# The Down product of a one-layer encoder block in Strassen form: a new table of visits in which no pair is read twice, and a last visit with evictions in an order of its own

## The chip, the cores and the metric

The kernel runs on one core of a Trainium2 chip. The metric is the device time of one execution in microseconds (us). Engines are called by their names in the profile: PE is TensorE's matmul, PEld its weight load, DVE VectorE, ACT ScalarE, POOL GpSimd and SP SyncE, which here only issues DMAs; a "q" behind a name (SPq) is that engine's queue of instructions.

## The reference

One layer over 512 tokens of width 2048, in float32. The part that matters is the last line of the layer and the final norm; the mixers and the attention to memory come before them and are not touched.

```python
for l in range(DEPTH):            # DEPTH is 1
    ...
    hm = rmsnorm(x, g_mlp[l])
    x = x + jnp.square(jax.nn.relu(hm @ w_up[l])) @ w_down[l]
return rmsnorm(x, g_final)
```

`w_up` is 2048 x 8192, `w_down` 8192 x 2048. Up is the first of the two products, Down the second.

## The kernel before, in words

All matmuls take float32 operands that were split in two float32r parts, hi and lo, and add three products of them (hi hi, hi lo, lo hi). The program is written by a planner: tasks are Python generators, each with a planned clock, and the order in which they issue on the five engines is fixed when the program is built (`step`, `until`, `spawn`). So each engine runs one written list in its order, and an instruction whose input is late holds up everything behind it on that engine.

Up and Down are both done in Strassen form with seven products instead of eight: `ORDER` names them p1, q6, p7, q4, p2, q5, p3. The work is cut in **units**, 128 for Up and 128 for Down. A unit has one weight block: three DMAs on SP (lines 1461 to 1465) and one DMA on POOL that adds onto what the first brought (line 1470), two adds of 256 columns on DVE, and the split of seven 256-column pieces by `hi_lo`: a cast on ACT (1024 columns, then 768) and a subtraction on DVE (the same two). Two such sets of pieces exist (`hl`), and four raw blocks (`ring`), so the weights of a unit are fetched four units ahead. PE then runs 7 products x 6 matmuls = 42 matmuls of 256 columns (`strassen_pe`, `one_product`, line 308); the first four products need the 1024 piece, the others the 768 one.

**Up** has 16 groups g of 8 units. After the last unit of a group `gen_up_out` takes the seven products out of their PSUM banks into the buffer `G`, squares and scales, forms the seven sums that Down needs (the rows of two **pairs**, 2g and 2g+1) in `G` as well, and writes them to `tp_dram` in DRAM (line 1598). The next group's evictions write `G` again, so they wait until these writes have read it.

**Down** contracts over 32 pairs for each of four output groups `ng`. The pairs come back from `tp_dram` by four DMAs of 224 KB each (`gen_load_t`, line 1646) into eight places of `big`, and are split there by one cast on ACT and one subtraction on DVE, both 128x1792. Since eight places hold eight pairs, Down goes in **visits** (ng, first pair, last pair): a visit runs one unit per pair, its seven products stay in seven of the eight banks, and at its end `gen_down_out` adds them into `CB[ng]`, which was loaded with the residual (`gen_load_res`, line 1669): one copy on ACT and eleven adds of 512 columns on DVE. While these run, the next visit's products take the banks in the order in which they come free. `pace(n)` behind a unit allows n more pair quarters to be fetched. Behind the ends of the last four visits (`FINAL`) `gen_square` squares the finished group on ACT and sums it on POOL, and `gen_out` does the final norm and the output. In the last visit q5 and p3 of all its pairs are put off to the end (`LATE`), from pieces kept in a free place of `big`; so a unit of the last visit has five products, 30 matmuls.

The visits of before have 4, 6, 8, then twelve of 8 pairs, then 2, 8 and 4; pairs 0 and 1 are read a second time as pairs 32 and 33, so 34 pairs are loaded (`NLOAD`).

## Time and profile before

| | us |
|---|---|
| median of 3 runs | 2350.24 (2349.97 to 2350.58) |
| the profiled execution | 2349.65 |
| its span, first to last instruction | 2347.9 |
| PE busy in the span | 2259.0 (96%) |
| DVE busy | 1681.3 (72%) |
| ACT busy | 1077.4 (46%) |
| mean granted clock of PE | 0.989 |

PE is busy for nearly the whole span, so what can be gained are its gaps and the time in which it runs at the lower clock. In a timeline a row has the start and the length in us, the engine, the line, what is written and read, the count of instructions that were merged, and in brackets the engine's idle time before it and what ended it.

### The profile page before, as it was taken

How to read it: one execution, taken by the hardware profiler on the slowest of the kernel's cores; microseconds unless marked ns; L12 is line 12 of the kernel's file. 1: busy time of each engine (PE TensorE's matmuls, PEld its weight loads, DVE VectorE, ACT ScalarE, POOL GpSimd, SP SyncE). 2: the span in 40 equal slices, each digit the busy share in tenths (PEclk: the TensorE clock that was granted, in tenths of full speed). 3: DMA queues.
4: the chain of work that ended last, by engine and by line, in shares of the span. 5: the costliest groups of instructions: out<-in, count | busy, mean ns of one | idle time of the engine just before them, and what ended most of it. 6: DMA issues, size and time to landing. Idle time of an engine off the chain costs nothing.

```text
span 2347.9 us, 41841 instructions
## 1 busy us (share of the span) xinstructions
PE 2259.0 (96%) x16056; PEld 2168.0 (92%) x16056; DVE 1681.3 (72%) x2645; ACT 1077.4 (46%) x1506; POOL 388.3 (17%) x477
## 2 busy tenths in 40 slices
PE   8999999999999999899999999998899999999986
PEld 8999999998888787799999999998899999999986
DVE  7678543447734557978687776877887878878777
ACT  6542433345533446654454544444444444444453
POOL 3110010113002101311111111111111111111131
PEclk9999999999999999999999999999999999999998
DMA  5323222231243434688878788789978888887963
GB/s 172 103 88 95 68 75 82 68 104 46 90 160 100 157 116 156 165 223 231 230 204 246 198 229 225 197 240 258 299 215 238 214 235 219 218 229 206 237 164 108
DMA packets 273770, 405.42 MB, mean 173 GB/s; under 512 B 24193, under 2 KB 176785, under 8 KB 273313
## 3 DMA queue, kind: packets, MB, share of 16 engines
q1 hardware_dynamic: 235392, 334.44, 44.0%
q0 software_dynamic: 36944, 67.21, 17.1%
q8 instruction: 125, 2.05, 0.3%
q10 hardware_dynamic: 1232, 1.09, 0.1%
q14 instruction: 77, 0.62, 0.1%
HBM read 364.90 MB, written 37.75 MB: 171 GB/s over the span
## 4 chain that ended last, share of the span: by engine, by line
PE 67%; DVE 15%; DMA 9%; issue 4%; POOL 2%; ACT 1%; SPq 1%; DVEq 0%; ACTq 0%; POOLq 0%
PE bank L308 34%; PE bank L303 31%; DVE fb L139 8%; DVE hl L139 5%; DMA tp_dram<-fb 3%; DMA fb<-in_w_up_dram 3%; DVE big L139 2%; PE bank L328 2%; POOL fb L139 2%; DMA fb<-in_w_dn_dram 1%; ACT hl L139 1%; DMA big<-tp_dram 1%; SPq L1463 0%; ACT fb L139 0%; SPq L1461 0%
## 5 line engine op out<-in xcount | busy, mean ns | idle before, releaser
L308 PE MATMUL bank<-big,hl 128*128 128x256 f32 x10704 | 1314.9, 285 | 55.1 <-DVE hl L139 26.2
L308 PEld LDWEIGHTS bank<-big,hl 128*128 128x128 f32 x10704 | 1300.6, 193 | 69.1 <-DVE hl L139 32.5
L139 ACT CAST hl<-fb 128x1024 fp32r<-128x1024 f32 (+4 forms) x699 | 641.1, 926 | 911.9 <-PE bank L308 369.3
L139 DVE TENSOR_TENSOR hl<-fb,hl 128x768 fp32r<-128x768 f32 (+5 forms) x698 | 746.4, 1082 | 426.1 <-ACT hl L139 425.4
L303 PE MATMUL bank<-hl,big 128*128 128x384 f32 (+4 forms) x2916 | 525.2, 330 | 8.0 <-ACT big L139 7.0
L303 PEld LDWEIGHTS bank<-hl,big 128*128 128x128 f32 x2916 | 479.4, 189 | 19.0 <-ACT big L139 7.0
L139 DVE TENSOR_TENSOR fb<-fb 128x256 f32<-128x256 f32 (+3 forms) x779 | 401.5, 526 | 84.3 <-DMA fb<-in_w_up_dram 57.8
L303 PE MATMUL bank<-big,hl 128*128 128x512 f32 (+1 forms) x1192 | 296.1, 390 | 0.0
L139 POOL TENSOR_TENSOR fb<-fb 128x128 f32<-128x128 f32 (+5 forms) x203 | 155.7, 788 | 710.0 <-ACT fb L139 286.2
L303 PEld LDWEIGHTS bank<-big,hl 128*128 128x128 f32 x1192 | 222.2, 188 | 43.3
L1470 POOL DMA_DIRECT2D fb<-in_w_dn_dram x128 | 110.6, 866 | 551.2 <-DMA fb<-in_w_dn_dram 196.7
L1470 POOL DMA_DIRECT2D fb<-in_w_up_dram x128 | 110.7, 865 | 540.1 <-DVE hl L139 211.3
L139 DVE TENSOR_TENSOR fb<-fb,bank 128x512 f32<-128x512 f32 x234 | 156.9, 682 | 42.3 <-DMA tp_dram<-fb 24.3
L139 ACT ACTIVATE fb<-fb 128x512 f32<-128x512 f32 (+2 forms) x144 | 116.6, 814 | 70.9 <-DVE fb L139 50.0
L303 PE MATMUL bank<-big 128*128 128x256 f32 (+2 forms) x534 | 113.2, 327 | 2.1 <-DVE big L139 1.2
L303 PEld LDWEIGHTS bank<-big 128*128 128x128 f32 x534 | 87.1, 188 | 10.1 <-DVE big L139 2.5
L139 ACT CAST big<-bank 128x512 fp32r<-128x512 f32 (+2 forms) x119 | 61.2, 540 | 56.6 <-PE bank L328 28.4
L139 ACT CAST big<-big 128x1792 fp32r<-128x1792 f32 x34 | 57.5, 1691 | 56.5 <-DMA big<-tp_dram 50.4
L139 DVE TENSOR_TENSOR big<-bank,big 128x512 fp32r<-128x512 f32 (+1 forms) x102 | 62.7, 642 | 25.5 <-ACT big L139 25.4
L139 DVE TENSOR_TENSOR big<-big 128x1792 fp32r<-128x1792 f32 x34 | 68.7, 2020 | 3.6 <-ACT big L139 3.6
L328 PE MATMUL bank<-cs,fb 128*128 128x128 f32 x384 | 60.2, 275 | 8.9 <-POOL fb L139 3.5
L328 PEld LDWEIGHTS bank<-cs,fb 128*128 128x128 f32 x384 | 46.3, 140 | 17.2 <-POOL fb L139 5.8
(90 smaller groups left out, 727.0 us busy)
## 6 DMA issues: line engine op xcount, KB each, us to landing
fb<-in_w_up_dram SPq DMA_DIRECT2D x256, 256.0 KB, 5.0
fb<-in_w_dn_dram SPq DMA_DIRECT2D x256, 256.0 KB, 4.9
fb<-in_w_up_dram POOLq DMA_DIRECT2D x128, 256.0 KB, 6.3
fb<-in_w_dn_dram POOLq DMA_DIRECT2D x128, 256.0 KB, 6.0
fb<-in_w_in_dram SPq DMA_DIRECT2D x80, 384.0 KB, 3.0
big<-tp_dram SPq DMA_DIRECT2D x136, 224.0 KB, 5.5
fb<-in_w_out_dram SPq DMA_DIRECT2D x32, 512.0 KB, 3.3
fb<-in_w_up_dram SPq DMA_DIRECT2D x128, 128.0 KB, 5.5
```

The costliest lines, as they stand in the source:

```text
L139: r = fn(*args, **kw)
L303: nc.tensor.matmul(out, lhsT, rhs, start=start, stop=stop)
L308: nc.tensor.matmul(out, lhsT, rhs, start=start, stop=stop, skip_group_check=True)
L328: nc.tensor.transpose(out, in_, ident)
L1470: nc.gpsimd.dma_start(s31, src[:, 256:768], accum_op=OP.add)
```

## The change

Four things are changed in Up's writes and in Down. The seven sums of an Up group are written to `tp_dram` by two DMAs of 896 KB, one behind the other, where before there were four (two of 512 KB and two of 384 KB) with a planned 4.5 us between them. The table of visits is another one, of 18 visits as before, and loads 32 pairs; the first visits have 4, 4, 6, 8, 6 and 8 pairs, the last four 10, 8, 4 and 6. The pace of the pair loads and of the residual loads is adapted. The last visit puts off two products of 6 pairs (before of 4), and has an eviction of its own (`gen_last_out`), in which the sums for the first half of the columns come first.

```diff
--- before.py
+++ after.py
@@ -1488,16 +1488,16 @@
         flag.add(("sa", i))
         while ("pe", i - 2) not in flag:
             yield 0
-        j = i - (nu - 4)
+        j = i - (nu - NLAST)
         if j < 0:
             yield from hi_lo(hi[:, 1024:1792], lo[:, 1024:1792], r[:, 1024:1792])
             flag.add(("sb", i))
             return
         yield from hi_lo(hi[:, 1536:1792], lo[:, 1536:1792], r[:, 1536:1792])
         flag.add(("sb", i))
-        while ("pe", nu - 11) not in flag:
-            yield 0
-        k = big[:, PAIR * 2 + 1024 * j : PAIR * 2 + 1024 * j + 1024]
+        while ("pe", first_s + 128 + sum(b - a for _, a, b in VISITS[:-3]) + 1) not in flag:
+            yield 0
+        k = big[:, 1024 * j : 1024 * j + 1024]
         yield from hi_lo(k[:, 0:512], k[:, 512:1024], r[:, 1024:1536])
         flag.add(("kept", j))
 
@@ -1592,12 +1592,8 @@
         sums([c(4), c(5), c(6), c(7)], c(0), c(1), c(2), c(3), dve)
         yield rt(G)
         x = G[:, 512:4096].rearrange("p (r m c) -> p r m c", r=7, m=2)
-        for a, b in ((0, 4), (4, 7)):
-            for m in range(2):
-                dst = tp_dram[2 * g + 1 - m][:, 256 * a : 256 * b].rearrange("p (r c) -> p r c", r=b - a)
-                nc.sync.dma_start(dst, x[:, a:b, m, :])
-                if g < 15:
-                    yield plan.clk["pe"] + 4500.0
+        for m in range(2):
+            nc.sync.dma_start(tp_dram[2 * g + 1 - m].rearrange("p (r c) -> p r c", r=7), x[:, :, m, :])
         flag.add(("t", g))
 
     def up_units(g):
@@ -1619,12 +1615,12 @@
 
 
 
-    VISITS = [(0, 0, 4), (1, 0, 6), (2, 0, 8)]
-    VISITS += [(v % 4, 2 * v - 4, 2 * v + 4) for v in range(3, 15)]
-    VISITS += [(1, 30, 32), (3, 26, 34), (0, 28, 32)]
+    VISITS = [(0, 0, 4), (1, 0, 4), (2, 0, 6), (3, 0, 8), (0, 4, 10), (1, 4, 12)]
+    VISITS += [(v % 4, 2 * v - 6, 2 * v + 2) for v in range(6, 14)]
+    VISITS += [(2, 22, 32), (3, 24, 32), (1, 28, 32), (0, 26, 32)]
     FINAL = (14, 15, 16, 17)
     LATE = ("q5", "p3")
-    NLOAD = 34
+    NLOAD, NLAST = 32, 6
     paced = [0]
 
     def pace(n):
@@ -1668,7 +1664,7 @@
                     src = xs_dram[n : n + 2, :, 256 * t : 256 * t + 256].rearrange("e p c -> p e c")
                     nc.sync.dma_start(dst.rearrange("p (e c) -> p e c", e=2), src)
                     plan.issue("dma", 100.0, [dst], [], 4000)
-                    yield plan.clk["pe"] + (1500.0 if ng == 0 else 4500.0)
+                    yield plan.clk["pe"] + (1500.0, 4500.0, 7000.0, 7000.0)[ng]
             flag.add(("res", ng))
 
     def gen_down_out(ng, st):
@@ -1716,6 +1712,42 @@
         free("p3")
         flag.add(("fin", id(st), 0, 1))
 
+    def gen_last_out(ng, st):
+
+        (c11, c12), (c21, c22) = CB[ng]
+        e, u2, u3 = (fslot(6144 + 512 * i) for i in range(3))
+        while not all(splits[nu - 1 - u].done for u in range(NLAST)):
+            yield 0
+
+        def add(dst, x, op=OP.add):
+            dve.tensor_tensor(dst, dst, x, op=op)
+
+        yield from product(st, "p1")
+        act.copy(e, st["p1"])
+        yield from product(st, "q6")
+        yield rt(e)
+        dve.tensor_tensor(u2, e, st["q6"], op=OP.subtract)
+        add(c11, e)
+        yield from product(st, "p7")
+        dve.tensor_tensor(u3, u2, st["p7"], op=OP.add)
+        yield from product(st, "q4")
+        add(c21, st["q4"], OP.subtract)
+        add(c21, u3, OP.subtract)
+        flag.add(("fin", id(st), 1, 0))
+        yield from product(st, "p2")
+        add(c11, st["p2"])
+        flag.add(("fin", id(st), 0, 0))
+        banks_f.put(*(st[r] for r in ORDER[:5]))
+        add(c22, u3, OP.subtract)
+        add(c12, u2)
+        yield from product(st, "q5")
+        add(c22, st["q5"])
+        flag.add(("fin", id(st), 1, 1))
+        add(c12, st["q5"], OP.subtract)
+        yield from product(st, "p3")
+        add(c12, st["p3"])
+        flag.add(("fin", id(st), 0, 1))
+
     def down_index(p, ng):
         if p < 28:
             return 16 * (p // 4) + 4 * ng + p % 4
@@ -1740,16 +1772,19 @@
                     elif v in FINAL:
                         spawn(gen_out(0, st), True)
                         spawn(gen_out(1, st), True)
-                    spawn(gen_down_out(ng, st), True)
+                    spawn(gen_down_out(ng, st) if v != FINAL[-1] else gen_last_out(ng, st), True)
                 strassen_pe(i, st, TP[s], j == 0, j == n - 1, ORDER[:5] if v == FINAL[-1] else ORDER)
                 if v == FINAL[-1] and j == n - 1:
                     until(lambda: ("kept", j) in flag)
                     for x, r in enumerate(LATE):
                         for u in range(n):
-                            k = big[:, PAIR * 2 + 1024 * u : PAIR * 2 + 1024 * u + 1024]
+                            k = big[:, 1024 * u : 1024 * u + 1024]
                             one_product(st, r, k[:, 0:512], k[:, 512:1024], 256 * x, TP[s0 + u],
                                         PRODUCTS[r][1], u == 0, u == n - 1)
-                pace(2 if v == 0 or (v == 1 and j < 2) else 1)
+                if v in (1, 2, 4, 14):
+                    pace((2 if j < 4 else 0) if v in (1, 14) else (2 if j < 2 else 1))
+                elif v > 0:
+                    pace(1)
             return run
 
         return [Unit(w_dn[down_index((s0 + j) % 32, ng)], 1024, pe(j)) for j in range(n)]
@@ -1785,7 +1820,7 @@
         sq = [fslot(4096 + 1024 * t + 512 * m) for m in range(2)]
         rs = rstd_l[:, 2 * t : 2 * t + 2]
         last = VISITS[FINAL[-1]][0]
-        while ("sqd", FINAL[-2]) not in flag or not all(splits[nu - 1 - u].done for u in range(4)):
+        while ("sqd", FINAL[-2]) not in flag or not all(splits[nu - 1 - u].done for u in range(NLAST)):
             yield 0
         b = None
         for x, m in enumerate((1, 0)):
```

The first place in the program is SP's list in the middle of an Up group. Its rows before, with the three DMAs of each unit's weights (lines 1461 to 1465) between the writes of `G`:

```order
L1598 DMA tp_dram<-fb 128x4x256 x2
L1461 DMA fb<-in_w_up_dram 128x2x256
L1463 DMA fb<-in_w_up_dram 128x512
L1465 DMA fb<-in_w_up_dram 128x256
L1461 DMA fb<-in_w_up_dram 128x2x256
L1463 DMA fb<-in_w_up_dram 128x512
L1465 DMA fb<-in_w_up_dram 128x256
L1598 DMA tp_dram<-fb 128x3x256
L1461 DMA fb<-in_w_up_dram 128x2x256
L1463 DMA fb<-in_w_up_dram 128x512
L1465 DMA fb<-in_w_up_dram 128x256
L1598 DMA tp_dram<-fb 128x3x256
```

and of the changed kernel at the same place:

```order
L1596 DMA tp_dram<-fb 896x1x256 x2
L1461 DMA fb<-in_w_up_dram 128x2x256
L1463 DMA fb<-in_w_up_dram 128x512
L1465 DMA fb<-in_w_up_dram 128x256
L1461 DMA fb<-in_w_up_dram 128x2x256
L1463 DMA fb<-in_w_up_dram 128x512
L1465 DMA fb<-in_w_up_dram 128x256
```

All 1792 KB of the group's sums now stand ahead of the weights of the units that follow; before, two writes of 384 KB stood behind the second and the third of these units.

The second place is DVE's list at the end of the second visit (rows `fb<-fb,bank` take a product out, rows `hl<-fb,hl` are the splits of a unit's weights, `fb<-fb 128x256 x2` the adds of one). Before, where that visit has 6 pairs:

```order
L139 TENSOR_TENSOR fb<-fb 128x512
L139 TENSOR_TENSOR fb<-fb,bank_64 128x512
L139 TENSOR_TENSOR fb<-fb 128x512
L139 TENSOR_TENSOR fb<-fb,bank_68 128x512
L139 TENSOR_TENSOR fb<-fb 128x512
L139 TENSOR_TENSOR fb<-fb,bank_63 128x512
L139 TENSOR_TENSOR fb<-fb 128x512
L139 TENSOR_TENSOR fb<-fb,bank_66 128x512
L139 TENSOR_TENSOR hl<-fb,hl 128x1024
L139 TENSOR_TENSOR fb<-fb,bank_70 128x512 x2
L139 TENSOR_TENSOR fb<-fb,bank_67 128x512
```

and of the changed kernel, where it has 4 (the first two adds of the eviction stand just ahead of these rows; `big<-big 128x1792` splits pair 4):

```order
L139 TENSOR_TENSOR fb<-fb 128x512
L139 TENSOR_TENSOR fb<-fb,bank_68 128x512
L139 TENSOR_TENSOR fb<-fb 128x512
L139 TENSOR_TENSOR fb<-fb 128x256 x2
L139 TENSOR_TENSOR fb<-fb,bank_63 128x512
L139 TENSOR_TENSOR fb<-fb 128x512
L139 TENSOR_TENSOR fb<-fb,bank_66 128x512
L139 TENSOR_TENSOR fb<-fb,bank_70 128x512 x2
L139 TENSOR_TENSOR fb<-fb,bank_67 128x512
L139 TENSOR_TENSOR fb<-fb 128x256 x2
L139 TENSOR_TENSOR big<-big 128x1792
L139 TENSOR_TENSOR hl<-fb,hl 128x1024
```

Before, the 1024 piece of the unit after next (the second of the new visit) stood behind the eighth add; now it stands behind all eleven, two pairs of adds for weights and the split of a pair. The splits of pairs 4 and 5, which stood behind the eviction of the first visit in the list of before, have moved here.

The third place is DVE's list where the last visit begins, with the eviction of the visit ahead of it. Before:

```order
L139 TENSOR_TENSOR fb<-fb 128x512
L139 TENSOR_TENSOR fb<-fb,bank_68 128x512
L139 TENSOR_TENSOR fb<-fb 128x512
L139 TENSOR_TENSOR fb<-fb,bank_63 128x512
L139 TENSOR_TENSOR fb<-fb 128x512
L139 TENSOR_TENSOR fb<-fb,bank_66 128x512
L139 TENSOR_TENSOR fb<-fb 128x512
L139 TENSOR_TENSOR fb<-fb,bank_70 128x512
L139 TENSOR_TENSOR hl<-fb,hl 128x1024
L139 TENSOR_TENSOR fb<-fb,bank_67 128x512 x2
L139 TENSOR_TENSOR fb<-fb,bank_69 128x512
```

and of the changed kernel (the first add of the eviction stands just ahead of these rows; `big<-fb,big` keeps a piece for the end):

```order
L139 TENSOR_TENSOR fb<-fb,bank_68 128x512
L139 TENSOR_TENSOR fb<-fb 128x512
L139 TENSOR_TENSOR fb<-fb,bank_63 128x512
L139 TENSOR_TENSOR fb<-fb 128x512
L139 TENSOR_TENSOR fb<-fb 128x256 x2
L139 TENSOR_TENSOR fb<-fb,bank_66 128x512
L139 TENSOR_TENSOR fb<-fb 128x512
L139 TENSOR_TENSOR big<-fb,big 128x512
L139 TENSOR_TENSOR fb<-fb,bank_70 128x512
L139 TENSOR_TENSOR fb<-fb,bank_67 128x512 x2
L139 TENSOR_TENSOR fb<-fb,bank_69 128x512
L139 TENSOR_TENSOR hl<-fb,hl 128x1024
```

Here too the 1024 piece has moved behind all eleven adds, and behind two more steps.

## Rows read from the trace of the kernel before

**Rows 1.** Stretch, length, busy of PE, PEld, DVE, ACT, POOL, PEclk, DMA share, GB/s.
```profile
1088.00:1592.00 504.00, 493.13 (x4053) 490.44 (x4051) 383.73 (x540) 240.16 (x266) 83.51 (x98) 0.99 0.83 221
1592.00:1750.00 158.00, 142.74 (x1130) 139.22 (x1129) 132.21 (x174) 75.42 (x76) 22.93 (x27) 0.98 0.91 262
...
2240.00:2327.00 87.00, 75.56 (x588) 73.76 (x587) 68.76 (x94) 43.99 (x72) 31.73 (x32) 0.94 0.44 107
```

**Rows 2.** PE's waits in these three stretches: total us, times, longest.
```profile
PE bank L308 <- DVE fb L139: 10.8, 10, 3.2
...
PE bank L308 <- DVE hl L139: 8.3, 6, 3.4
PE bank L308 <- DVE fb L139: 6.9, 10, 1.8
...
PE bank L308 <- DVE hl L139: 9.2, 4, 5.6
PE bank L308 <- DVE fb L139: 1.6, 3, 0.6
```

**Rows 3.** The same columns as rows 1, in 8 us at the end of an Up group.
```profile
1463.00:1471.00 8.00, 6.49 (x31) 6.49 (x32) 6.99 (x11) 4.48 (x6) 0.86 (x1) 0.57 0.48 92
```

**Rows 4.** Timeline around the end of that Up group, SPq, DVE and PE.
```profile
1441.21 0.98 SPq L1598 DMA_DIRECT2D tp_dram<-fb  x2
...
1460.21 0.89 DVE L139 TENSOR_TENSOR fb<-fb 128x256 f32<-128x256 f32 x2 [3.45 <-DMA fb<-in_w_up_dram]
...
1463.77 1.48 DVE L139 TENSOR_TENSOR fb<-fb,bank 128x512 f32<-128x512 f32 x2 [2.67 <-DMA tp_dram<-fb]
...
1464.51 1.86 PE L308 MATMUL bank<-big,hl 128*128 128x256 f32 x7 [3.16 <-DVE fb L139]
```

**Rows 5.** DVE's waits in the first stretch, 1088 to 1592 us.
```profile
DVE fb L139 <- DMA fb<-in_w_up_dram: 49.1, 34, 3.4
...
DVE fb L139 <- DMA tp_dram<-fb: 24.3, 12, 4.1
```

**Rows 6.** DMAs issued near 1385, 1441, 1446, 1626: count, size, us to landing.
```profile
fb<-in_w_up_dram SPq DMA_DIRECT2D x2, 256.0 KB, 3.5
...
tp_dram<-fb SPq DMA_DIRECT2D x2, 512.0 KB, 5.9
...
fb<-in_w_up_dram SPq DMA_DIRECT2D x2, 256.0 KB, 7.3
...
tp_dram<-fb SPq DMA_DIRECT2D x1, 384.0 KB, 9.6
```

**Rows 7.** Timeline where Down begins: DVE, ACT and PE.
```profile
1635.34 1.48 DVE L139 TENSOR_TENSOR fb<-fb,bank 128x512 f32<-128x512 f32 x2 [5.73 <-DMA big<-tp_dram]
...
1668.99 2.02 DVE L139 TENSOR_TENSOR big<-big 128x1792 fp32r<-128x1792 f32 x1
...
1671.75 1.69 ACT L139 CAST big<-big 128x1792 fp32r<-128x1792 f32 x1 [9.60 <-DMA big<-tp_dram]
...
1672.20 4.06 PE L308 MATMUL bank<-big,hl 128*128 128x256 f32 x20 [3.44 <-DVE hl L139]
```

**Rows 8.** Timeline at the end of a later visit: first add, eighth's follower, PE.
```profile
2236.29 0.69 DVE L139 TENSOR_TENSOR fb<-fb 128x512 f32<-128x512 f32 x1
...
2241.92 1.22 DVE L139 TENSOR_TENSOR hl<-fb,hl 128x1024 fp32r<-128x1024 f32 x1
...
2244.39 1.81 PE L308 MATMUL bank<-big,hl 128*128 128x256 f32 x13 [0.45 <-DVE fb L139]
```

**Rows 9.** Timeline where the last visit begins: first add, next 1024 piece.
```profile
2298.05 0.68 DVE L139 TENSOR_TENSOR fb<-fb 128x512 f32<-128x512 f32 x1
...
2303.71 1.22 DVE L139 TENSOR_TENSOR hl<-fb,hl 128x1024 fp32r<-128x1024 f32 x1
```

**Rows 10.** Timeline of the tail: sums of squares on PE, first scalings on DVE.
```profile
2326.82 4.93 PE L303 MATMUL bank<-ones,fb 128*128 128x2 f32 x40
...
2332.32 3.67 DVE L139 TENSOR_TENSOR fb<-fb,bank 128x512 f32<-128x512 f32 x6 [0.37 <-PE bank L328]
```

## The prediction, made before the changed kernel was run

> **What bounds the kernel now.** I read the busy times by stretch first, then PE's waits in each, then the timeline at the places where the longest stand. PE is busy for 493.13 of 504 us in Up's main part, 142.74 of 158 where Down begins, 75.56 of 87 at the end [rows 1]. Up's 4053 matmuls in 493.13 us give 0.122 us each, so a unit of 42 takes 5.1 us. What is lost there stands in PE's waits [rows 2]: 10.8 us in ten gaps in Up, 8.3 + 6.9 = 15.2 where Down begins, 9.2 + 1.6 = 10.8 at the end. All are put down to DVE: "DVE hl" means that the split of a unit's weights was late, "DVE fb" that a bank was not yet taken out. With a long gap the granted clock goes to half: in the 8 us around one it is 0.57 and PE makes 31 matmuls [rows 3], which at 0.122 us are 3.8 us of work in the 6.5 us after the gap, so 2.7 lost. DVE is 76% busy in Up but 84% (132.21 of 158) where Down begins [rows 1], so there a gap is not only a wait but a lack of DVE time. I make the sum against the profiled execution, 2349.65 us, which is 0.6 under the median of the three runs.
>
> **Up's writes.** The ten gaps of Up stand at group ends. At the one of 3.16 us DVE's row that takes out the next products had waited 2.67 us for a write of the group before, and just ahead of it an add of weights 3.45 us for its DMA [rows 4]. Over the stretch DVE waited 24.3 us in 12 such waits for writes, 2.0 each, and 49.1 us in 34 for weights [rows 5]; the latter delayed no split that PE stood waiting for, since every wait of PE there is for a bank.
>
> In the new list all 1792 KB are issued where the first 1024 KB were, at 1441.21 [rows 4]. The two of 512 KB landed in 5.9 us [rows 6]. The other 768 KB go at 221 GB/s over a share of 0.83, 266 GB/s, the rate of a full queue [rows 1], so 3.0 us more: everything has landed by about 1451. The group's matmuls ended at 1464.51 - 3.16 = 1461.35, so its last unit began near 1456.2, and nothing writes the buffer before. The waits for writes should be gone.
>
> The price is that weights issued behind the burst come later. Weights with nothing in front landed in 3.5 us, those behind the two writes of before in 7.3 [rows 6]. By the time that the adds at 1460.21 got theirs, three of the four old writes had landed and the fourth was on its way, so against before only 384 KB or less are new in front of them: 0 to 1.5 us; I take 1.2. The mean group end then gains 2.0 - 1.2 = 0.8 us on DVE against a gap of 10.8/10 = 1.08; 0.3 us stays, 3 us in all. Up gains 10.8 + 2.7 - 3 = **10.5 us**; at most 13.5. If the full 3.0 us of the added bytes reached the adds, each gap would grow by 1.0 instead: 10 us lost. The Trainium skill says it harder (DMA: Bandwidth & Descriptors, Queues, rings and completion order): an SDMA engine takes the descriptors of one ring in their order, and SP's DMAs all share a row of rings. The 7.3 against 3.5 us agree. Read so that all later weights keep the whole delay, it gives the 10 us of loss, and with the other terms below about 2352.
>
> That the write is one of 896 rows costs nothing I can see: its pieces stay 1 KB, and the bytes are the same.
>
> **Where Down begins.** First, the same writes: DVE waited 5.73 us at 1635.34 [rows 7], until the last write of 384 KB, issued near 1626, had taken 9.6 us [rows 6]. Its bytes now go some 14 us earlier, but ahead of a half of pair 1, whose split then comes later in DVE's list. I take 3 of the 5.7 us; 0 and 5.7 are the bounds. Second, the splits of pairs 4 and 5 leave the list behind the first eviction. ACT sat 9.60 us before pair 4 with the next unit's cast behind it, DVE's split of a pair takes 2.02, and PE had its gap of 3.44 there [rows 7]: 2 us gained, at most 3.4.
>
> Third, the end of the second visit. The first add of an eviction follows the first of the seven products of the last unit, after ACT's copy, so it comes some 3.3 us before the visit ends, and the 1024 piece of the new visit's second unit is needed 5.1 us after that: 8.4 us behind the first add. Before, eight adds and the piece took 2241.92 + 1.22 - 2236.29 = 6.9 us, and only the banks cost 0.45 [rows 8]. Now eleven adds of 0.70 (7.7), two pairs of adds for weights (1.8), a split of 2.0 and the piece (1.2) make 12.7: 4.3 us late. The ten bank waits of this stretch are 6.9 us [rows 2], some 1.5 of it at the old end of that visit, so +2.8. Fourth, there are two more visit ends in the stretch, 0.45 each: +0.9. Half-clock spells I leave as they are. Sum -3 - 2 + 2.8 + 0.9 = **-1.3 us**, between -9 and +5.
>
> **The end.** The visit of 2 pairs lasts 10.2 us and holds an eviction (7.7) and the DVE work of two units, some 3 us each (1.2 + 1.0 for the splits, 0.9 for the adds), 13.7 in all, with its own eviction behind it and the split of a repeated pair, 2.0, ahead: hence the gap of 5.6 [rows 2]. The shortest visit is now 4 units, 20.4 us against 7.7 + 12.4, which fits. But a unit of the last visit has 30 matmuls, 3.7 us, so the second one needs its 1024 piece 3.3 + 3.7 = 7.0 us behind the first add. Before it was ready after 2303.71 + 1.22 - 2298.05 = 6.9 [rows 9]. Now eleven adds, a pair of adds for weights, a kept piece of 0.7 and the split make 7.7 + 0.9 + 0.7 + 1.2 = 10.5: 3.5 late, and the next 0.5 more. So of today's 10.8 us of gaps and some 3.5 at half clock (the granted mean of 0.94 over 87 us [rows 1], less what falls into gaps) there come back 4.0, a half-clock spell of 2.7 and three visit ends of 0.45, 8.0: **-6.3 us**, between -12 and +1. The two pairs that are no longer read save 8 DMAs and 3.7 us each of ACT and DVE; outside the short visit these lay beside matmuls and give nothing.
>
> **The tail.** The last q5 and p3 are now of six pairs; that is work moved from ahead of the tail into it, at no cost. The sums of squares for the first half of the columns, 20 of the 40 rows in 4.93 us [rows 10], and its transposes go between these products: +3.2 on PE. In return half of the sums and the first half's ten scalings, 3.67 us for six [rows 10] and about 1.6 for four, no longer stand behind the last product; but DVE's add of that product stands behind the scalings, which start only 2.9 us before the product ends. I take **0**, between -5 and +3.
>
> Sum: -10.5 - 1.3 - 6.3 = -18.1; 2349.65 - 18.1 = 2331.6, with the median's 0.6 some 2332. Since most terms are taken nearer their costly bound, I say **2330 us**.
>
> **Rivals.** (1) Weights starve Up. If the burst's 3.0 us reach PE within each of the 15 groups, 45 us are added to the sum: 2331.6 + 45 = 2377. It is slower than before from 1.2 us per group on (15 x 1.2 = 18, the sum of all gains). For it: DVE waits for weights 34 times as it is [rows 5]. Against: four units are fetched ahead, and waits up to 3.4 us cost no matmul. Chance 0.07. (2) Only Up gains: what the new table saves at the short visit it gives back at the second and the last; 2349.65 - 10.5 = 2339. For it: DVE does the same work where Down begins, less 4 us. Chance 0.2. (3) All goes: Up -13.5, Down's begin -7, the end -11: 2318. It asks that DVE's rows run with less delay than I counted, as where casts come early. Chance 0.17. (4) It changes nothing that counts: weights take the place of the writes as the last wait at group ends (Up 0), the end as in (2): about 2349; chance 0.06. My forecast, 2324 to 2336: 0.5.
>
> **Numbers.** The range takes in forecast, (2) and most of (3): 2316 to 2344. Within 0.2% (4.7 us, about what a measurement can tell from no change) lies (4) and the upper edge of (2), 0.08; slower by more (1) with 0.06; faster 0.86.
>
> **What would show it.** Up: no DVE wait for its writes at group ends, PE's waits under 5 us for 10.8, writes landing within some 10 us. Down's begin: DVE's first take-out near 1632 of this trace's time base, less what Up gave; ACT's wait before pair 4 gone; a gap of 3 to 4 us in the first unit after the second visit. The end: no gap at a short visit, one of some 3.5 us at the second unit of the last visit. It is wrong if PE waits for "DVE hl" within Up's groups, or if the gaps at the two places do not come.

## The result, and the profile after

The changed kernel took 2331.6 us (median of three runs, 2326.64 to 2335.12) against 2350.24 before: a ratio of 0.9919, with a 95% interval of 0.9889 to 0.9948. The forecast was 2330 us. The profiled execution is the longest of the three: 2335.12 us, span 2333.3.

The first view is PE's waits in the three stretches of [rows 2], here 1088 to 1593, 1593 to 1750 and 2215 to 2315 us.

```profile
PE bank L308 <- DVE fb L139: 5.2, 4, 1.9
PE bank L308 <- DVE hl L139: 0.4, 1, 0.4
...
PE bank L308 <- DVE hl L139: 8.4, 4, 3.4
PE bank L308 <- DVE fb L139: 3.6, 6, 1.1
...
PE bank L308 <- DVE hl L139: 3.8, 2, 3.2
PE bank L308 <- DVE fb L139: 1.0, 2, 0.5
```

The waits in Up fell from 10.8 to 5.6 us. Where Down begins they fell from 15.2 to 12.0 (over the same units, the second stretch of the table below, only from 16.0 to 15.4), and the four for a unit's pieces ("DVE hl") are as long as the six of before. At the end 4.8 us are left of 10.8. DVE's waits in Up answer to [rows 5]:

```profile
DVE fb L139 <- DMA fb<-in_w_up_dram: 72.9, 36, 5.1
DVE hl L139 <- ACT hl L139: 34.4, 42, 1.3
```

No wait for a write is left, and 24.3 us of them were there before. But the waits for weights grew by 23.8 us, from 49.1: the waiting time was exchanged, not removed. PE gained because of where it now falls. The timeline around one group's writes and the longest wait of PE in Up shows this (SPq, DVE, PE):

```profile
1521.08 1.39 SPq L1596 DMA_DIRECT2D tp_dram<-fb  x2
1523.73 1.72 SPq L1461 DMA_DIRECT2D fb<-in_w_up_dram  x1
...
1528.42 1.18 SPq L1461 DMA_DIRECT2D fb<-in_w_up_dram  x1
...
1540.66 0.89 DVE L139 TENSOR_TENSOR fb<-fb 128x256 f32<-128x256 f32 x2 [4.95 <-DMA fb<-in_w_up_dram]
1541.47 1.47 DVE L139 TENSOR_TENSOR fb<-fb,bank 128x512 f32<-128x512 f32 x2
...
1542.20 4.09 PE L308 MATMUL bank<-big,hl 128*128 128x256 f32 x22 [1.92 <-DVE fb L139]
```

The take-outs at 1541.47 wait for no write; it is the add of weights ahead of them that comes late. I split the 72.9 us by the unit that PE is in. Six of the 36 waits, 22.9 us, stand in the first unit of a group, where the take-outs are; before, such waits were two, 6.7 us, beside the twelve waits for writes. So weights now hold DVE up at six of the twelve group ends, where the writes did at all twelve, and PE waits at four ends instead of ten. The other 50.0 us fall between ends, where only one of them cost PE anything (0.36 us). The one shown fell on an end and cost 1.92 us.

Next, the second visit's end, on DVE, with PE's wait below: the eviction's first add, the two adds of weights, a pair's split, the pieces.

```profile
1672.87 0.68 DVE L139 TENSOR_TENSOR fb<-fb 128x512 f32<-128x512 f32 x1
...
1681.08 0.88 DVE L139 TENSOR_TENSOR fb<-fb 128x256 f32<-128x256 f32 x2
...
1681.87 2.02 DVE L139 TENSOR_TENSOR big<-big 128x1792 fp32r<-128x1792 f32 x1
...
1683.81 2.09 DVE L139 TENSOR_TENSOR hl<-fb,hl 128x1024 fp32r<-128x1024 f32 x2
...
1685.08 2.29 PE L308 MATMUL bank<-big,hl 128*128 128x256 f32 x9 [3.44 <-DVE hl L139]
```

This is the gap of 3 to 4 us that the prediction put there. In the 11 us around it the granted clock is 0.71 (the windows view, columns as in [rows 1]):

```profile
1679.00:1690.00 11.00, 7.56 (x44) 7.25 (x43) 10.83 (x14) 3.46 (x3) 0.99 (x2) 0.71 0.74 209
```

The last visit's second unit, and the tail (DVE and PE):

```profile
2271.56 0.69 DVE L139 TENSOR_TENSOR fb<-fb 128x512 f32<-128x512 f32 x1 [0.52 <-ACT fb L139]
...
2280.41 1.74 DVE L139 TENSOR_TENSOR hl<-fb,hl 128x1024 fp32r<-128x1024 f32 x1
...
2282.21 7.97 PE L308 MATMUL bank<-big,hl 128*128 128x256 f32 x44 [3.20 <-DVE hl L139]
...
2312.11 3.12 PE L308 MATMUL bank<-big 128*128 128x256 f32 x24
...
2312.39 3.67 DVE L139 TENSOR_TENSOR fb<-fb,bank 128x512 f32<-128x512 f32 x6 [1.22 <-PE bank L328]
2315.99 1.65 DVE L139 SCALAR_TENSOR_TENSOR fb<-fb,gn,bank 128x256 f32<-128x256 f32 x4
2317.55 0.68 DVE L139 TENSOR_TENSOR fb<-fb,bank 128x512 f32<-128x512 f32 x1
```

The piece is ready 10.6 us behind the first add (2280.41 + 1.74 - 2271.56) where 10.5 was forecast. In the tail the last product ends at 2315.2, and its add stands behind ten scalings until 2317.55.

For all kernels of this study I split the profiled execution at the same units, counting 42 matmuls of L308 to a unit: Up from unit 24 to 122; Down's begin from there over Down's first 37 units; the next 71 units, steady; the end, to the start of the last such matmul; the tail from there to the end of the span. All times are us.

| kernel | Up | Down's begin | steady | end | tail | span | median of runs |
|---|---|---|---|---|---|---|---|
| before | 512.0 | 241.7 | 367.1 | 117.8 | 21.2 | 2347.9 | 2350.2; 2351.0, 2349.1, 2349.7, 2350.8 beside the experiments |
| after | 504.4 | 242.6 | 366.3 | 113.2 | 18.4 | 2333.3 | 2331.6 |
| writes alone | 505.6 | 237.6 | 366.8 | 120.1 | 21.0 | 2337.3 | 2338.4 |
| table alone | 510.0 | 243.5 | 366.4 | 113.3 | 18.4 | 2340.2 | 2341.5 |
| four unspaced | 501.9 | 238.8 | 366.8 | 121.3 | 21.3 | 2338.9 | 2337.4 |
| after again | 503.0 | 244.2 | 366.4 | 113.2 | 18.5 | 2332.2 | 2331.8 |
| short visit back | 501.2 | 243.5 | 371.9 | 116.5 | 18.4 | 2337.6 | 2343.3 |
| short visit gone | 511.2 | 240.2 | 370.3 | 118.9 | 21.9 | 2349.0 | 2351.5 |
| old last order | 501.9 | 243.2 | 366.4 | 112.9 | 20.4 | 2329.7 | 2332.4 |
| writes doubled | 582.5 | 246.9 | 366.7 | 112.1 | 18.0 | 2420.7 | 2420.2 |
| short gone, paced | 511.2 | 240.4 | 374.9 | 111.4 | 22.3 | 2346.4 | 2350.4 |
| tail and paces | 501.3 | 242.3 | 366.5 | 113.2 | 17.2 | 2326.5 | 2330.5 |
| two writes spaced | 508.0 | 241.8 | 366.5 | 112.6 | 18.4 | 2336.3 | 2330.5 |
| splits moved | 506.3 | 242.6 | 366.4 | 117.8 | 14.9 | 2334.3 | 2327.4 |

### The profile page after: what moved, and what is told of

Read it like the earlier page. It is cut to its first block, busy times and chain, and to the rows that moved or that the text cites. A ratio compares the mean times of both kernels' runs of the same rounds, so it can differ in the third digit from the quotient of the medians.

```text
span 2333.3 us, 41775 instructions
## 1 busy us (share of the span) xinstructions
PE 2261.2 (97%) x16056; PEld 2172.6 (93%) x16056; DVE 1677.6 (72%) x2645; ACT 1072.0 (46%) x1506; POOL 387.0 (17%) x477
## 3 DMA queue, kind: packets, MB, share of 16 engines
q0 software_dynamic: 36944, 67.21, 17.2%
## 4 chain that ended last, share of the span: by engine, by line
PE 68%; DVE 15%; DMA 8%; issue 5%; POOL 2%; ACT 1%; SPq 0%; DVEq 0%; POOLq 0%; ACTq 0%
PE bank L308 34%; PE bank L303 32%; DVE fb L139 8%; DVE hl L139 5%; DMA fb<-in_w_up_dram 5%; DVE big L139 2%; DMA fb<-in_w_dn_dram 2%; PE bank L328 2%; POOL fb L139 2%; DMA big<-tp_dram 1%; ACT hl L139 1%; ACT big L139 0%; DMA tp_dram<-fb 0%; ACT fb L139 0%; DVE small L139 0%
## 5 line engine op out<-in xcount | busy, mean ns | idle before, releaser
L308 PE MATMUL bank<-big,hl 128*128 128x256 f32 x10680 | 1309.4, 285 | 40.8 <-DVE hl L139 20.4
L308 PEld LDWEIGHTS bank<-big,hl 128*128 128x128 f32 x10680 | 1297.6, 193 | 52.3 <-DVE hl L139 26.2
L139 ACT CAST hl<-fb 128x1024 fp32r<-128x1024 f32 (+5 forms) x699 | 639.2, 924 | 930.2 <-PE bank L308 348.0
L303 PEld LDWEIGHTS bank<-hl,big 128*128 128x128 f32 x2916 | 481.0, 190 | 18.6 <-ACT big L139 6.3
L139 DVE TENSOR_TENSOR fb<-fb 128x256 f32<-128x256 f32 (+3 forms) x779 | 402.3, 527 | 118.9 <-DMA fb<-in_w_up_dram 85.9
L139 DVE TENSOR_TENSOR fb<-fb,bank 128x512 f32<-128x512 f32 x234 | 156.6, 682 | 15.8 <-PE bank L308 2.9
## 6 DMA issues: line engine op xcount, KB each, us to landing
fb<-in_w_out_dram SPq DMA_DIRECT2D x32, 512.0 KB, 3.3
```

The costliest lines, as they stand in the source:

```text
L139: r = fn(*args, **kw)
L303: nc.tensor.matmul(out, lhsT, rhs, start=start, stop=stop)
L308: nc.tensor.matmul(out, lhsT, rhs, start=start, stop=stop, skip_group_check=True)
```

## The experiments

**The two halves of the change.** The kernel before with the new writes, and the kernel after with the old ones:

```
writes alone (before.py):
-        for a, b in ((0, 4), (4, 7)):
-            for m in range(2): ... yield plan.clk["pe"] + 4500.0
+        for m in range(2):
+            nc.sync.dma_start(tp_dram[2 * g + 1 - m].rearrange("p (r c) -> p r c", r=7), x[:, :, m, :])
table alone (after.py): the same edit in reverse
```

> The kernel before with Up's two writes of 896 KB in place of the four spaced ones, and nothing else. Theory (the terms of the prediction are separate): Up gives 10.5 us, and the two bursts of the last groups 3 us at Down's first take-out, so 2350.2 - 13.5 = 2337 us, between 2334 and 2341; the waits of PE in Up fall from 10.8 us to about 5 as in the trace of after, and the waits where Down begins and at the end (8.3 + 6.9 and 10.8 us) stay within 3 us of before. Rival (weights take the place of the writes as what ends last at a group's end, and the table gave the whole gain): 2347 to 2352 us. Rival (weights starve Up): slower than 2352.

> The kernel after with Up's four spaced writes back, so the table of visits, the last visit's own order and the paces of loads alone. Theory (the terms are separate): where Down begins the table brings +1.7 (-2 + 2.8 + 0.9), the end -6.3, the tail 0 by the prediction, -2.8 by the trace of after; so 2350.2 - 4.6 = 2345.6, or 2343 with the tail; PE's waits in Up are back at some 10 us. Rival (the two help each other: the shorter first visits ask for pairs earlier, and late writes hold those up): a wait for the splits of pairs 0 to 7 where Down begins, and 2350 us or more. Rival (the table alone gives the whole gain): 2333 us.

Measured: writes alone 2338.38 us, ratio 0.9951 (0.9936 to 0.9966), -12.6 us where -13.5 was expected. Table alone 2341.52, ratio 0.9965 (0.9950 to 0.9980), -9.4 us where -4.6 to -7 was expected. Both together are -19 us, less than the sum of 22. The rivals fall: neither half is the whole, and weights do not starve Up. PE waited 7.3 us in Up with the new writes and 11.0 with the old ones, where DVE's waits for writes were back (24.6 us in 11). In the table Down's begin is about 2 us shorter with the writes alone (237.6, 238.8 against 240.2 to 241.7) and about 3 longer with the visits alone.

**Spacing or row length.** The four old writes, without the 4.5 us between them:

```
-                if g < 15:
-                    yield plan.clk["pe"] + 4500.0
```

> The kernel before with its four writes per group (512, 512, 384, 384 KB) issued one behind the other, without the 4.5 us between them; rows as before. Theory (what counts is when the bytes are issued, not the length of the rows): the same as with two writes, within 2 us, so about 2337. Rival (the longer rows or the fewer DMAs count): 3 us or more slower than with two writes, in gaps of PE at group ends.

Measured: 2337.36 us, ratio 0.9948 (0.9932 to 0.9964), 1 us from the two long writes. So the time of issue counts, not the rows.

**The kernel after once more**, unchanged.

> The kernel after once more, for the width of its runs (2326.6 to 2335.1 in three) and a second profile. Theory (the width is that of short gaps which just do or do not send the granted clock to half, some 3 us each): runs between 2325 and 2336 with a median near 2331; the gaps of 3.0, 3.4 and 3.2 us at the end of Up's last group, behind the second visit and in the last visit's second unit stand in this profile too, and what differs is one to three spells of half clock at other places. Rival (one of the three large gaps comes and goes): it is missing here when the run is faster.

Measured: 2331.79 us (2329.37 to 2333.94, six runs), ratio 0.9924 (0.9909 to 0.9939). The three large gaps stand in this profile too. That the width is one of half-clock spells is not shown: already the first matmul of Up starts between 948.9 and 951.4 us in the fourteen profiles, though everything ahead of it is the same program.

**The short visit, put back and taken away.**

```
short visit back (after.py), visits from the fourteenth on:
-    ... (1, 20, 28), (2, 22, 32), (3, 24, 32), (1, 28, 32), (0, 26, 32)
+    ... (1, 20, 30), (2, 22, 32), (3, 24, 32), (1, 30, 32), (0, 26, 32)
short visit gone (before.py):
-    ... (1, 22, 30), (2, 24, 32), (1, 30, 32), (3, 26, 34), (0, 28, 32)
+    ... (1, 22, 28), (2, 24, 32), (1, 28, 32), (3, 26, 34), (0, 28, 32)
```

> The kernel after with a visit of 2 pairs again at the end: the visits from the fourteenth are 10, 10, 8, 2, 6 pairs in place of 8, 10, 8, 4, 6; work, writes and the last visit stay. Theory (the end gained by the short visit going, where an eviction and two units' splits don't fit into 10.2 us of matmuls): the gap of some 5.6 us is back in the unit behind the short visit, with a half-clock spell a loss of 9 to 10.6 us there as in the trace of before, of which the 0.7 us of an ordinary visit end and some of the last visit's own gap (the eviction ahead of it comes later) count against it: 7 to 10 us, 2339 to 2342 us against 2331.8. Rival (the end gained by the last visit's length and its kept pieces): 2331 to 2334 us.

> The kernel before with one thing changed: the visits of 8 and 2 pairs over the same columns become 6 and 4. Theory: the jam at the short visit (10.6 us beyond its matmuls in the trace of before) shrinks to a visit end of 0.7 and at most one more gap of 1 to 2; the last visit stays as it was (5.1 us lost in its second unit). So 7 to 10 us faster than before: 2341 to 2344 against 2351. Rival (the gap only moves to the next place where DVE is behind): within 3 us of before.

Measured: back 2343.32 us, ratio 0.9978 (0.9966 to 0.9990), 11.5 slower than after; gone 2351.48, ratio 1.0012 (0.9999 to 1.0024), no gain at all. The first looks as expected and is not quite. In it half of pair 30 is loaded over pair 22 (it has landed by 2170.60 us, and the visit that begins with pair 22 starts at 2172.40), so its result is not that of the layer and only its times are used; and of its loss some 5.5 us stand in the steady stretch (371.9), where PE waited 2.4 and 1.5 us for the split of a pair that my longer visit needs sooner. To the end itself belong 3.3 us (116.5 against 113.2), with a gap of 4.1 us at the second unit of the last visit, where after has 3.2. The second contradicts the theory. Its timeline shows where the gain went (DVE, then PE, at two visit ends):

```profile
2233.44 2.34 DVE L139 TENSOR_TENSOR big<-big 128x1792 fp32r<-128x1792 f32 x1
...
2237.02 2.62 DVE L139 TENSOR_TENSOR hl<-fb,hl 128x1024 fp32r<-128x1024 f32 x2
...
2238.30 22.10 PE L308 MATMUL bank<-big,hl 128*128 128x256 f32 x168 [4.29 <-DVE hl L139]
...
2259.04 2.47 DVE L139 TENSOR_TENSOR big<-big 128x1792 fp32r<-128x1792 f32 x1
...
2264.50 44.05 PE L308 MATMUL bank<-big,hl 128*128 128x256 f32 x348 [4.11 <-DVE hl L139]
```

At both ends a pair's split of 2.3 to 2.5 us stands between the eviction and the piece that PE waits for. These are splits of the pairs that this table reads twice. In the kernel before they stand elsewhere: that of pair 33 in the short visit, that of pair 32 (the first row below, DVE) in the sixth unit of a long visit, through which PE ran without a wait (the second):

```profile
2227.06 2.02 DVE L139 TENSOR_TENSOR big<-big 128x1792 fp32r<-128x1792 f32 x1
...
2203.04 40.90 PE L308 MATMUL bank<-big,hl 128*128 128x256 f32 x336 [0.45 <-DVE fb L139]
```

That gave a new theory: what costs is a pair's split on a visit's end.

**That theory, tested**: the same kernel with the last pairs' loads issued earlier.

```
-                pace(2 if v == 0 or (v == 1 and j < 2) else 1)
+                pace((2 if j < 4 else 0) if v in (13, 14) else 2 if v == 0 or (v == 1 and j < 2) else 1)
```

> The kernel before with the short visit gone as in the run before (6 and 4 pairs in place of 8 and 2), and the loads of pairs 30 to 33 issued by the fourth unit of the last two long visits instead of one piece per unit to their end. That run gained nothing: its trace has gaps of 4.3 and 4.1 us in the second units behind two visit ends, each with a pair's split (2.3 to 2.5 us of DVE) between the eviction's adds and the piece that PE waits for. Theory (a pair's split that falls on a visit's end is what costs, not the length of a visit alone): both gaps go, 6.0 + 6.3 us beyond the matmuls become some 1.5, and the time is 2339 to 2344 us against 2349 to 2351 before. Rival (the pairs read twice or the length of the last visits cost by themselves): within 3 us of before.

Measured: 2350.40 us, ratio 1.0004 (0.9993 to 1.0015), no gain. But the end itself went from 118.9 to 111.4 us, while the stretch ahead of it grew from 370.3 to 374.9. Both are in the trace (DVE and PE):

```profile
2235.26 1.22 DVE L139 TENSOR_TENSOR hl<-fb,hl 128x1024 fp32r<-128x1024 f32 x1
...
2237.72 21.76 PE L308 MATMUL bank<-big,hl 128*128 128x256 f32 x176 [0.45 <-DVE fb L139]
2262.00 8.20 PE L308 MATMUL bank<-big,hl 128*128 128x256 f32 x54 [2.51 <-DVE hl L139]
...
2189.45 2.02 DVE L139 TENSOR_TENSOR big<-big 128x1792 fp32r<-128x1792 f32 x1
...
2192.72 1.31 PE L308 MATMUL bank<-big,hl 128*128 128x256 f32 x8 [2.15 <-DVE fb L139]
2195.44 4.85 PE L308 MATMUL bank<-big,hl 128*128 128x256 f32 x21 [1.41 <-DVE hl L139]
```

Without a split on it the first of the two visit ends costs 0.45 us for 4.29; a split (of pair 31) now fell on the end of the visit before, and waits of 2.15 and 1.41 us with it. So at this end what stands ahead of the piece is shown to cost. It is not the split alone: with it gone, the last three adds of the eviction and two adds of weights stand behind the piece as well. The second end has no split left either and still costs 2.51 us of 4.11. A table gains from this only if it moves splits away from every end; the forecast of the total was wrong.

**The last visit's order.**

```
-                    spawn(gen_down_out(ng, st) if v != FINAL[-1] else gen_last_out(ng, st), True)
+                    spawn(gen_down_out(ng, st), True)
```

> The kernel after with the last visit's eviction in the common order again (one buffer e shared with the squares, eleven adds as in the other visits) in place of the order of its own. Theory (the prediction's tail term: the new order moves work that hides behind 60 late matmuls): within 2 us of after. Rival (the shared buffer e holds the first adds up until the squares of the visit before are summed): 2 to 6 us slower than after, all of it behind the last visit's first products.

Measured: 2332.38 us, ratio 0.9934 (0.9919 to 0.9948), 0.6 over after. In the trace end and tail together are 133.3 against 131.6 us: the new order is worth 1.7 us by the profiles and 0.6 by the medians, both within the width of the runs.

**Twice the burst.**

```
+        for m in range(2):
+            nc.sync.dma_start(tq_dram[2 * g + 1 - m].rearrange("p (r c) -> p r c", r=7), x[:, :, m, :])
```

> The kernel after, and behind each group's two writes two more of the same 1792 KB into a scratch tensor: twice the burst. This prices what a burst does to the weights behind it. In the trace of after DVE's waits for writes in Up are gone (24.3 us before) but its waits for weights went from 49.1 to 72.9 us, and PE waited 5.6 us: the added delay fell where PE had banks to spare. Theory (the weights' delay is the price and has a break-even): another 6.7 us per burst, 1792 KB at 266 GB/s, cannot all be taken up, and each group loses 1 to 5 us: 2347 to 2407 us, with PE's waits in Up at 12 to 60 us, behind adds of weights. Rival (nothing hangs on the burst, the whole of it hides behind the four units fetched ahead): within 4 us of after.

Measured: 2420.2 us, ratio 1.0304 (1.0283 to 1.0326). Up took 582.5 us against 502.4, the median of the eight kernels with the single burst: 80 us over 98 units, 12.25 groups, 6.5 each, above the 1 to 5 that were expected and nearly the whole time of the added bytes (6.7 by the estimate). The timeline of one group (SPq, DVE, PE):

```profile
1400.91 0.38 SPq L1462 DMA_DIRECT2D fb<-in_w_up_dram  x1
...
1402.32 1.75 SPq L1597 DMA_DIRECT2D tp_dram<-fb  x2
1404.12 6.63 SPq L1599 DMA_DIRECT2D tq_dram<-fb  x2
1410.86 3.05 SPq L1462 DMA_DIRECT2D fb<-in_w_up_dram  x1
...
1428.02 0.88 DVE L139 TENSOR_TENSOR fb<-fb 128x256 f32<-128x256 f32 x2 [8.23 <-DMA fb<-in_w_up_dram]
...
1429.55 42.71 PE L309 MATMUL bank<-big,hl 128*128 128x256 f32 x336 [5.08 <-DVE fb L139]
```

The first 1792 KB cost PE little, the next 1792 KB nearly their full time. The added writes read `G` too, but DVE had no wait for them between 1100 and 1600 us, against 95.9 us for weights. So I read it that one burst uses up the units fetched ahead.

**Spaced again, but in two.**

```
+            if g < 15 and m == 0:
+                yield plan.clk["pe"] + 4500.0
```

> The kernel after with 4.5 us between a group's two writes of 896 KB, so that weights can go between them; in the last group there is no space, as before. Theory (the burst's price is the delay of the weights right behind it, and the writes only have to land by the end of the next group's matmuls): DVE's waits for weights in Up fall below the 72.9 us of after, PE's waits there stay at or under 5 us, and the gap of 3.0 us in the sixth unit of the last group, where weights landed 6 to 7.5 us behind the burst, shrinks; 0 to 4 us faster than after. Rival (the later second write is waited for again, as in the kernel before): DVE's waits for writes are back and it is 2 to 5 us slower than after.

Measured: 2330.51 us, ratio 0.9920 (0.9902 to 0.9939), the same as after. Both forecasts of the mechanism miss: waits for weights were 78.0 us in 41, and none for writes. PE waited 8.2 us in eight in Up, not 5 or less. But this profile, with its 508.0 us of Up, is of the longest of its six runs, 2338.1; by the medians there is nothing to choose between one burst and two halves 4.5 us apart. That the last write starts 9 us earlier than in the kernel before, by the planned spaces, seems to be enough, which no run tried by itself.

**Two attempts at a better version.**

```
tail and paces (after.py), loads per unit in the second to fourth visit, and in gen_out:
+  1: (2, 2, 0, 0), 2: (2, 2, 2, 2, 0, 0), 3: (2, 2, 2, 2, 1, 1, 1, 1)
+        while t == 0 and ("fin", id(st), 0, 1) not in flag:
+            yield 0
```

> The kernel after with two edits far apart in time, read apart in the trace. First, the scalings of the output's first half wait until the last product's add: in the trace of after that add starts at 2317.55, behind 5.3 us of scalings, while the product ended at 2315.1. Theory: the add and all behind it come 2.2 to 2.4 us earlier, and the scalings fit into the 5.5 us in which DVE then waited. Rival: the scalings push the second half's, 0. Second, the loads of pairs 5 to 7 are issued in the first units of a visit only (2, 2, 0, 0; 2, 2, 2, 2, 0, 0; 2, 2, 2, 2, 1, ...), so that no pair's split falls between the second visit's eviction and the 1024 piece of the unit behind it. Theory: the gap of 3.44 us there and the half clock behind it, 6.0 us beyond the matmuls, shrink to 1 to 3. Rival (where Down begins DVE lacks time in sum): the gap moves to the next visit's end and nothing is gained. Both theories: 2324 to 2328 us against 2331.7; the tail alone 2329.5.

Measured: 2330.45 us, ratio 0.9919 (0.9901 to 0.9937). The tail is 17.2 against 18.4 us: 1.2 gained, not 2.3, as the eleven rows now pushed back the second half's root of the mean. The paces gave nothing. Pair 4's loads went earlier, but its split stayed where it was, behind the eviction, and the gap is 3.44 us again. So the last kernel moved the splits themselves:

```
splits moved (after.py; second visit's loads now 4, 0, 0, 0):
+            while s in (4, 6) and ("sb", first_s + 128 + {4: 9, 6: 15}[s]) not in flag:
+                yield 0
+        while j == 0 and ("sa", i + 1) not in flag:        # first kept piece
+            yield 0
+            while t == 0 and ng == VISITS[FINAL[2]][0] and ("fin", id(st), 0, 1) not in flag:
+                yield 0
```

> The kernel after with three edits, each read at its own place. (a) Where Down begins, the splits of pairs 4 and 6 wait until the second unit behind a visit's end has its pieces, and the loads are issued so that they are there by then: in all traces so far a gap of 1.4 to 4.3 us stood where a pair's split lay within a visit's end. Theory: the 6.0 us lost behind the second visit become 2 or less, since 2.0 of the 3.44 us of the gap go and a shorter gap need not bring the clock down. Rival (DVE lacks time in sum there): the loss stands at the next visit's end. (b) In the last visit the first kept piece (0.68 us) comes behind the second unit's first piece: the gap of 3.2 us becomes 2.5. (c) The scalings of the output's first half for the last two visits, and only these, wait for the last product's add. Theory: the add comes 2.3 us earlier and nothing is pushed back, where the form before gave 1.2. Sum by theory: 4 + 0.7 + 2.3 = 7, 2325 us against 2331.7; with the rival in (a) 2329.

Measured: 2327.38 us (2325.47 to 2327.78, and the profiled run 2336.07), ratio 0.9896 (0.9879 to 0.9913). It is the fastest of all, 4 us under after, though the two intervals touch. By place (DVE and PE behind the second visit; PE four units on; DVE in the last visit):

```profile
1680.85 2.08 DVE L139 TENSOR_TENSOR hl<-fb,hl 128x1024 fp32r<-128x1024 f32 x2
1682.85 2.02 DVE L139 TENSOR_TENSOR big<-big 128x1792 fp32r<-128x1792 f32 x1
1682.12 18.13 PE L308 MATMUL bank<-big,hl 128*128 128x256 f32 x149 [1.65 <-DVE hl L139]
...
1705.23 7.02 PE L308 MATMUL bank<-big,hl 128*128 128x256 f32 x44 [2.82 <-DVE big L139]
...
2295.26 0.88 DVE L139 TENSOR_TENSOR fb<-fb 128x256 f32<-128x256 f32 x2 [4.02 <-DMA fb<-in_w_dn_dram]
```

(a) The split now stands behind the pieces, in a list that is the same up to there, and the gap behind the second visit fell from 3.44 to 1.65 us: this is the clean price of one split, 1.8 us of PE for 2.0 of DVE. But 2.82 us of waiting for pair 5 came four units later: the rival. (b) The gap in the last visit fell from 3.20 to 2.08 us, but the deferred piece held its buffer of weights, and DVE waited 4.02 us for the unit that is loaded into it (the load four units on waits for all splits of this one, and SP issued it at 2285.45 us, where after does at 2277.94); the end took 117.8 us against 113.2, a loss in this profile. The profile is of the longest of the four runs, 8 us above the next; of the other three there is no trace, so whether they lost as much there is open. (c) The tail is 14.9 against 18.4, a gain of 3.5 where 2.3 was expected.

## Why the prediction was right, and where it was not

**Up's writes, -10.5.** By the table -8.8 (502.4 against 511.2, medians of the eight kernels with both writes at once and the four with the old ones). The waits for writes went, as said, and they landed within 6.9 and 10.1 us of their issue in the group shown. The price on the weights was sized nearly right: 1.2 us per group end were taken, and in the first units of groups DVE's waits for weights grew by (22.9 - 6.7) / 12 = 1.35 us (0.9 and 1.45 in the profiles of after again and of writes alone). DVE waited 23.8 / 12 = 2.0 us more per group in all, and the rest of that fell between ends. What I had wrong in kind is the mean group end: 0.3 us were to stay at each, 3 in all, and what stayed is 5.2 us at four ends and nothing at the others. Of the signs of being wrong one came in part: PE did wait for "DVE hl" within groups, once 0.36 us, and 3.00 in Up's last group:

```profile
1611.37 4.87 PE L308 MATMUL bank<-big,hl 128*128 128x256 f32 x26 [3.00 <-DVE hl L139]
```

The kernel before has 2.13 us at the same place, and the second profile of the changed kernel 2.02, so this is not shown to come from the longer burst. Rival (1) had the right mechanism; its break-even lies between one and two bursts.

**Where Down begins, -1.3.** By the table it became some 3 us longer (the four kernels with after's program there have 242.6 to 244.2, the three of before 240.2 to 241.7). Its steps came as written: the first take-out at 1624.65 without a wait, ACT's wait ahead of pair 4's cast 1.55 us for 9.60, the gap of 3.44 behind the second visit. The row of 5.73 us, which I read as a wait for the last write, names a load of a pair; with the new table and the old writes it is back, 5.94 us, and names the write. The step that failed is the addition. The writes alone gave about -2 and the visits alone about +3, for -3 and +1.7 forecast; together nothing of the writes' gain is left. Two costs had no term. The end of the fifth visit costs PE four waits, 2.3 us in sum, in the trace of after, where an ordinary end costs 0.45. And the time beyond waits and matmuls (at 0.12 us each), the half-clock spells that I left as they are among it, went from 9.7 to 10.5 us (medians of the three and the four kernels). That work which comes earlier runs into the same lack of DVE time a few units on is my reading; no run tested it.

**The end, -6.3, and the tail, 0.** The forecast gap in the last visit came (3.5 said, 3.20 measured), and none at a short visit. By the table end and tail together gave -9.5 (131.6, the median of the three kernels with after's program there, against 141.1, of the three with that of before). The 20 small matmuls that moved ahead of the last product, 2.3 us, only pass from the tail to the end in this count; without them the end gave 9.2 us and the tail 0.5 (medians of each), so the tail's 0 was near. The end's term is too small for a reason of its own: it was added up from one profile, and that one has 117.8 us there, where the two others of the same program have 120.1 and 121.3. Against that profile the gain is 6.9 us.

The sentence that the pairs no longer read give nothing outside the short visit is not refuted: in the kernel before pair 32's split cost PE nothing, and pair 33's stands in the short visit. What I had not seen is that the two halves of the table's change need each other. With the short visit gone and the pairs still read twice, their splits moved onto two visit ends and nothing was gained; with the loads earlier 7.5 us left the end and 4.6 came back in the stretch ahead of it. With the short visit back and no pair read twice, end and tail took 134.9 us, 3.3 above after and 6.2 under before, at the price of a longer visit ahead. So how the 9.5 us divide between the short visit and the pairs stays open, and that -6.3 fits the one profile so well is in part luck.

The parts forecast too small, the end, and too large, Up and Down's begin, cancel in part: -8.8 + 2.9 - 0.4 (steady, 366.4 against 366.8) - 9.5 = -15.8, for -18.1 said and -18.6 measured between the medians. I can place the remaining 2.8 us nowhere; the spans of the two profiles are 14.6 us apart, and the three runs of the changed kernel differ by 8.5. So that the total was met this closely, while Down's begin had the wrong sign, is luck as well.

## What to carry to other kernels

Where one engine's list is served in order, cost a change by what stands in that list between the last free moment and the instruction that is waited for: behind the second visit here, a split of 2.0 us moved out of that place took 1.8 us off PE's gap. A burst of transfers is cheap only as far as the work fetched ahead of it lasts, so double it once to see how near its edge is. Gains at two places that are limited by the same engine a few units apart need not add; where Down begins they did not.

## What the runs showed of the hardware

Issuing DMAs takes SP longer behind a large burst, so the price of one is paid in the issuing queue too. The DMA of a unit's first weights takes it 0.38 us in the median of Up, and 0.38 behind the 1024 KB of the kernel before. Behind 1792 KB it takes 0.4 to 3.7 us (median 1.0 over the 16 bursts of after, 1.72 in the group shown), behind 3584 KB 2.2 to 4.4 (median 3.0 over the 16 of the kernel with writes doubled, 3.05 in the group shown).
